# Matmul with batch norm on one core: the shift column, the fifth tile's first blocks and the last tile's first chunk

## The chip, the cores and the metric

The kernel runs on one core of a Trainium2 chip. A core has a matrix engine (TensorE, PE in the profile), three engines for elementwise work (VectorE or DVE, ScalarE or ACT, GpSimd or POOL), a queue engine that issues transfers (SyncE, SP) and 16 DMA engines that move data between memory and the core. SBUF is the core's working memory, and PSUM the memory of eight banks into which TensorE writes. The metric is the device time of one execution in microseconds (us); lower is better.

## The reference

```python
y = np.matmul(x, weight)                       # x: 16 x 512 x 1024, weight: 1024 x 768
mean = np.mean(y, axis=(0, 1), keepdims=True)  # over all 8192 rows, one value per column
var = np.var(y, axis=(0, 1), keepdims=True)
y_norm = (y - mean) / np.sqrt(var + eps)
return (gamma * y_norm + beta).astype(np.float32)
```

No output can be written before the mean and the variance of its column are known, that is, before all 8192 rows of that column are multiplied. The output is 8192 x 768 floats, 25.17 MB.

## The kernel before, in words

The 768 columns are six tiles of 128, counted `nt` = 0 to 5 (`NT` = 6), and the 8192 rows are 16 chunks of 512, counted `c` (`C` = 16). While x is loaded, the first three tiles (`GA` = 3) are computed for all chunks, and tiles 3, 4 and 5 for the first five chunks (`EARLY` = 5). Once x is in, tiles 3, 4 and 5 follow one after the other for chunks 5 to 15 (line 579 on): eight matmuls of 128 x 512 for each chunk (`mm`, line 196). This is the part that the change touches.

In tiles 3 to 5 a product lies with the columns of y on the partitions. For each chunk VectorE takes the statistics from PSUM (`bn`, line 318) and ScalarE copies the product to SBUF as bf16 (`keep`, line 345). Both read the same bank, and ScalarE's copy waits for VectorE's statistics. When a tile's last chunk is through, `finish_var` (lines 352 to 354) and `finish_affine` (lines 358 to 363) make the tile's scale and shift: VectorE aggregates, ScalarE takes the root, VectorE the reciprocal, ScalarE makes scale and shift by three operations of one element per partition, and, in line 363, copies the shift to a spare column of a PSUM bank. That bank (`a_ps`, line 270) also holds the scale row that VectorE multiplies the first three tiles with (`norm_rows`, line 285). Tile 3 has column 384 of the bank and tile 4 column 385.

Then the outputs of the tile (`outputs`, line 547) go through in blocks of two chunks (b = 0 to 7):

- `norm` multiplies by scale and adds shift in place. It has three forms. "act" is one ScalarE activation (line 381). "dve" is a VectorE `tensor_scalar` (line 392). "dve1" is a VectorE `scalar_tensor_tensor` that reads the shift from the PSUM column (line 387). While GpSimd still works on the first three tiles' rows (`shift_rows`, line 291), the even chunk of a block goes to ScalarE and the odd one to VectorE as "dve1"; later blocks are all "dve".
- `turn_y` queues eight 128 x 128 transposes on TensorE (line 408). Inside the matmul loop one waiting transpose is issued after each matmul (`turn_one`), and whatever is left when the block is copied out is issued in one burst (`out_copy`).
- `out_copy` has ScalarE copy the transposed block from PSUM to SBUF as float (line 421), and `store` issues a 512 KB store on SyncE's queue (line 426).

Tile 4's last block is held back (`HELD` = 1) until tile 5's matmuls are issued. Tile 5, the last, is finished by `finish` (line 366). Its chunks then go out one by one (`last_outputs`, line 568): normalise on VectorE, four transposes, one ScalarE copy of 128 x 512, one store of 256 KB.

The order of the work on each engine is fixed when the program is built. `at(t, fn, ...)` notes a step with a planned time, the list is sorted by these times, and `seq` chains the instructions of each engine in that order. An instruction that waits therefore holds everything that stands behind it on its engine. The planned times are no measurement; they only set the order. The framework adds the waits between engines from what each instruction reads and writes.

Of the kernel before, what the change touches and what calls it, by code (L numbers as in the profile page):

```python
# [10 lines left out]
def kernel(  # L11
# [23 lines left out]
    nc = tc.nc  # L35
# [3 lines left out]
    ALU = mybir.AluOpType  # L39
# [5 lines left out]
    P = 128  # L45
    NT = N // P
    KQ = K // 4
    CH = 512
    RT = CH // P
    C = M // CH  # L50
    QR = 256
    QPC = CH // QR
# [5 lines left out]
    GA = 3  # L58
    COLS = (0, 5, 10, 15)
    NA = GA * P  # L60
# [16 lines left out]
    def seq(bi):  # L77

        ins = bi.ins
        prev = last.get(ins.engine)  # L80
        if prev is not None:
            tc.add_manual_dep(
                ins, prev,
                mybir.DependencyInfo(mybir.DependencyClass.NoSync, mybir.DependencyReason.DATA),
                reason="order",
            )
        last[ins.engine] = ins.name
        return bi
# [6 lines left out]
    scale = singles.tile([P, NT], f32)  # L95
    shift = singles.tile([P, NT], f32)
# [30 lines left out]
    xs, xT, py, ygrp, yrow, ops, ost, aff = {}, {}, {}, {}, {}, {}, {}, {}  # L127
# [140 lines left out]
    def spread_rows(i):  # L268

        a_ps = psum.tile([P, CH], f32, tag="b")  # L270
        aff[i] = a_ps[:, 0:NA]
        if i == 0:
            aff["shift"] = a_ps[:, NA:NA + NT - GA]
        seq(nc.tensor.matmul(aff[i], full, aff["diag"][:, i], start=True, stop=True))  # L274
        if i == 1:
            seq(nc.scalar.copy(sum1, aff[i]))  # L276
# [24 lines left out]
    def y(nt, c):  # L301
        key, i = ((nt, c // GY), c % GY) if nt >= GA else ((0, c), nt)
        if key not in ygrp:
            y_sb = ypool.tile([P, GY, CH], bf16, tag="y")
            ygrp[key] = y_sb
        return ygrp[key][:, i]
# [49 lines left out]
    def finish_affine(nt):  # L356
        one = slice(nt, nt + 1)
        seq(nc.scalar.activation(nscale, rstd, AF.Identity, scale=ngamma[:, one]))
        seq(nc.scalar.activation(scale[:, one], rstd, AF.Identity, scale=gamma_sb[:, one]))
        seq(nc.scalar.activation(  # L360
            shift[:, one], mv[:, nt, 0:1], AF.Identity, bias=beta_sb[:, one], scale=nscale))
        if nt < NT - 1:
            seq(nc.scalar.copy(aff["shift"][:, nt - GA:nt - GA + 1], shift[:, one]))

    def finish(nt):
        one = slice(nt, nt + 1)
# [12 lines left out]
    def norm(nt, c, eng):  # L379
        if eng == "act":  # L380
            seq(nc.scalar.activation(  # L381
                y(nt, c), y(nt, c), AF.Identity,
                bias=shift[:, nt:nt + 1], scale=scale[:, nt:nt + 1],
            ))
        elif eng == "dve1":

            seq(nc.vector.scalar_tensor_tensor(  # L387
                y(nt, c), y(nt, c), scale[:, nt:nt + 1],
                aff["shift"][:, nt - GA:nt - GA + 1].to_broadcast([P, CH]), op0=ALU.mult, op1=ALU.add,
            ))  # L390
        else:
            seq((nc.vector if eng == "dve" else nc.gpsimd).tensor_scalar(  # L392
                y(nt, c), y(nt, c), scale[:, nt:nt + 1], shift[:, nt:nt + 1],
                op0=ALU.mult, op1=ALU.add,
            ))

    def turn_y(nts, m0, tiles):

        o_ps = psum.tile([P, tiles, len(nts), P], bf16, tag="b")
        ops[nts, m0] = o_ps  # L400
        for s in range(tiles):
            c, i = divmod(m0 // P + s, RT)
            for a, nt in enumerate(nts):
                turns.append(((nts, m0), o_ps[:, s, a], y(nt, c)[:, i * P:(i + 1) * P]))
# [30 lines left out]
    def at(t, fn, *args):  # L435
        events.append((t, len(events), fn, args))
# [85 lines left out]
    at(S + 0.9, affine_rows)  # L522
    at(S + 2.4, shift_diag)
    at(S + 4.4, spread_rows, 0)
    at(S + 5.6, spread_rows, 1)
    for nt in range(GA):
        at(S + 5.0, norm, nt, 0, "dve")
    ga = tuple(range(GA))
    tr, tk = S + 4.7, S + 6.3
    for c in range(C):  # L530
        if c in COLS:
            for nt in range(GA):
                if c:
                    at(tk - 3.4 + 0.8 * nt, norm, nt, c, "act")
            for s in range(0, RT, 2):
                at(tk + 0.7 * s, turn_y, ga, c * CH + s * P, 2)
                at(tk + 0.7 * s + 1.9, out_copy, ga, c * CH + s * P, "act")
                at(tk + 0.7 * s + 2.7, store, ga, c * CH + s * P, 2)
            tk += 9.6 if c else 7.2
        else:  # L540
            for s in range(0, RT, 2):
                at(tr, norm_rows, c, s)
                at(tr + 1.1, shift_rows, c, s)
                at(tr + 3.0, store_rows, c, s)
                tr += 1.85

    def outputs(nt, t0, step):
        for b in range(C // 2):
            tb = t0 + step * b
            if nt == NT - 2 and b >= C // 2 - HELD:  # L550
                held.append(b)
                continue
            for i in range(2):
                at(tb - 2.2 + 0.5 * i, norm, nt, 2 * b + i, "dve" if tb > tr + 2.0 else "dve1" if i else "act")
            at(tb, turn_y, (nt,), 2 * b * CH, 2 * RT)
            at(tb + 2.2, out_copy, (nt,), 2 * b * CH, "act")
            at(tb + 2.3, store, (nt,), 2 * b * CH, 2 * RT)
# [10 lines left out]
    def last_outputs(nt, t0):  # L568

        for c in range(C):  # L570
            tb = t0 + 0.6 * c
            at(tb - 1.2, norm, nt, c, "dve")
            at(tb, turn_y, (nt,), c * CH, RT)
            at(tb + 0.5, out_copy, (nt,), c * CH, "act", True)
            at(tb + 0.6, store, (nt,), c * CH, RT)
# [3 lines left out]
    for nt in range(GA, NT):  # L579
        for c in range(EARLY, C):  # L580
            if (nt, c) == (NT - 1, C - 1):
                for q in range(QPC):
                    at(pe, mm_half, q)
                    pe += 0.9
                    at(pe + 0.2, bn_half, q)
                    at(pe + (0.4 if q == 0 else 1.0), keep_half, q)
                at(pe - 2.4, sum_up)
                continue
            for jws in halves:
                unit(nt, c, MM_US / 2 + (0.12 if nt == GA else 0.17), jws)  # L590
        if nt < NT - 1:
            at(pe + 0.55, finish_var, nt)
            at(pe + 1.6, finish_affine, nt)
        else:
            at(pe + 0.55, finish, nt)
        if nt == GA:
            outputs(nt, S + 37.0, 2.3)
        elif nt < NT - 1:
            outputs(nt, pe + 4.6, 1.85)
        else:  # L600
            held_outputs(nt - 1, pe)
            last_outputs(nt, pe + 3.0)
# [39 lines left out]
```

## Time and profile before

| | us |
|---|---|
| four runs | 217.39, 217.95, 218.10, 218.62; median 218.03 |
| the profiled execution | 217.39, its span 215.6 |
| PE busy in the span | 200.8 (93%) |
| DVE busy | 152.2 (71%) |
| POOL busy | 133.8 (62%) |
| ACT busy | 120.6 (56%) |
| loading and the first three tiles' matmuls | to about 124 |
| tiles 3 to 5, the rest of their matmuls | to about 197 |
| after the last matmul to the end of the span | about 18 |

The span is from the first to the last instruction; 1.79 us of the profiled execution lie around it. A busy PE is not a PE at its peak, since matmuls overlap. What counts in the stretch from 124 to 197 us is the distance between the starts of the PE's instructions: 0.28 us for a matmul of 128 x 512 with a transpose behind it. In the last 18 us the DMA engines write the last tile. The profile gives starts, durations and, in brackets, how long an engine sat idle ahead of an instruction and which instruction released it.

### The profile page before, as it was taken

How to read it: one execution, taken by the hardware profiler on the slowest of the kernel's cores; microseconds unless marked ns; L12 is line 12 of the kernel's file. 1: busy time of each engine (PE TensorE's matmuls, PEld its weight loads, DVE VectorE, ACT ScalarE, POOL GpSimd, SP SyncE). 2: the span in 40 equal slices, each digit the busy share in tenths (PEclk: the TensorE clock that was granted, in tenths of full speed). 3: DMA queues.
4: the chain of work that ended last, by engine and by line, in shares of the span. 5: the costliest groups of instructions: out<-in, count | busy, mean ns of one | idle time of the engine just before them, and what ended most of it. 6: DMA issues, size and time to landing. Idle time of an engine off the chain costs nothing.

```text
span 215.6 us, 3455 instructions
## 1 busy us (share of the span) xinstructions
PE 200.8 (93%) x1178; PEld 106.4 (49%) x1178; DVE 152.2 (71%) x263; ACT 120.6 (56%) x229; POOL 133.8 (62%) x153
## 2 busy tenths in 40 slices
PE   7998999999999999999999999999999999996900
PEld 2453555554544566645656544444445545554900
DVE  3222868897988789998754449988999949838800
ACT  2001463654553466645666423867768977996950
POOL 7788677779684699962558402999999943000000
PEclk9999999999999999999999999999999999999675
DMA  4999999999999999996000000598789998999997
GB/s 55 170 200 182 196 196 192 197 194 195 196 190 194 197 196 196 196 197 83 0 5 0 0 0 0 204 383 310 287 297 367 362 338 283 303 347 325 303 345 233
DMA packets 70161, 43.75 MB, mean 203 GB/s; under 512 B 4096, under 2 KB 69632, under 8 KB 70144
## 3 DMA queue, kind: packets, MB, share of 16 engines
q0 software_dynamic: 34624, 18.36, 62.1%
q1 hardware_dynamic: 35520, 25.18, 36.1%
q8 instruction: 9, 0.15, 0.3%
q14 instruction: 8, 0.07, 0.1%
HBM read 36.71 MB, written 25.17 MB: 287 GB/s over the span
## 4 chain that ended last, share of the span: by engine, by line
PE 78%; ACT 5%; DMA 5%; DVE 3%; POOL 3%; issue 1%; ACTq 0%; POOLq 0%
PE y_ps L196 43%; PE y_ps L186 29%; PE o_ps L408 4%; ACT o_sb L421 3%; DMA w_sb<-in_weight_dram 3%; DMA ring<-in_x_dram 2%; POOL w_sb L149 2%; POOL ring L162 1%; ACT ring L421 1%; PE y_ps L332 1%; ACT y_sb L381 1%; DVE stats L318 1%; DVE y_sb L387 1%; PE a_ps L274 1%; PE tot_ps L232 1%
## 5 line engine op out<-in xcount | busy, mean ns | idle before, releaser
L196 PE MATMUL y_ps<-xT_sb,w_sb 128*128 128x512 bf16 (+1 forms) x484 | 117.5, 382 | 1.1 <-DMA w_sb<-in_weight_dram 0.8
L196 PEld LDWEIGHTS <-w_sb 128*128 128x128 bf16 x484 | 46.0, 96 | 59.2 <-issue 2.7
L345 ACT CAST y_sb<-y_ps 128x512 bf16<-128x512 f32 x59 | 35.1, 595 | 51.3 <-DVE stats L318 48.4
L186 PE MATMUL y_ps<-w_sb,xT_sb 128*128 128x384 bf16 x384 | 63.4, 326 | 0.0
L162 POOL DMA_DIRECT2D ring<-in_x_dram x72 | 45.2, 634 | 12.5 <-DVE xT_sb L174 6.5
L318 DVE BATCH_NORM_STATS2 stats<-y_ps 128x6 f32<-128x512 f32 x58 | 39.1, 685 | 17.6 <-PE y_ps L196 17.6
L186 PEld LDWEIGHTS <-xT_sb 128*128 128x128 bf16 x384 | 37.6, 98 | 25.6
L174 DVE STREAM_TRANSPOSE xT_sb<-ring 128x1024 f32<-128x1024 f32 (+1 forms) x34 | 39.5, 1170 | 14.3 <-DMA ring<-in_x_dram 14.2
L212 POOL TENSOR_TENSOR sum<-sum,sq_sb 128x384 f32<-128x384 f32 x38 | 38.1, 1002 | 17.4 <-ACT sq_sb L208 15.9
L408 PE MATMUL o_ps<-ident,y_sb 128*128 128x128 bf16 x240 | 38.8, 230 | 2.1 <-DVE y_sb L392 1.7
L291 POOL TENSOR_TENSOR ring<-ring,sum 128x768 f32<-128x768 f32 x17 | 31.0, 1847 | 12.1 <-ACT sum L276 12.1
L215 DVE TENSOR_TENSOR sum<-y_ps,sum 128x384 f32<-128x384 f32 x48 | 26.1, 545 | 13.9 <-ACT sq_sb L208 12.9
L208 ACT ACTIVATE sq_sb<-y_ps 128x384 f32<-128x384 f32 x48 | 23.5, 494 | 13.8 <-PE y_ps L186 10.5
L221 ACT CAST y_sb<-y_ps 128x384 bf16<-128x384 f32 x48 | 22.9, 478 | 9.4 <-DVE sum L215 9.2
L421 ACT CAST ring<-o_ps 128x1024 f32<-128x1024 bf16 (+1 forms) x24 | 22.9, 972 | 4.4 <-PE o_ps L408 2.3
L408 PEld LDWEIGHTS <-y_sb 128*128 128x128 bf16 x240 | 21.0, 103 | 5.5 <-DVE y_sb L392 1.8
L285 DVE TENSOR_TENSOR ring<-y_sb,a_ps 128x768 f32<-128x768 bf16 x17 | 15.9, 939 | 0.0
L291 POOL TENSOR_TENSOR o_sb<-o_sb,sum 128x768 f32<-128x768 f32 x7 | 12.8, 1833 | 4.0 <-DVE o_sb L285 4.0
L381 ACT ACTIVATE y_sb<-y_sb,shift,scale 128x512 bf16<-128x512 bf16 x17 | 13.5, 816 | 0.0
L392 DVE TENSOR_SCALAR y_sb<-y_sb,scale,shift 128x512 bf16<-128x512 bf16 x35 | 12.5, 421 | 0.0
L155 PE MATMUL idle_ps<-idle_sb 128*128 128x512 bf16 x38 | 11.0, 458 | 1.2 <-DVE idle_sb L103 1.2
L421 ACT CAST o_sb<-o_ps 128x512 f32<-128x512 bf16 x16 | 7.9, 673 | 0.3 <-PE o_ps L408 0.3
(64 smaller groups left out, 56.2 us busy)
## 6 DMA issues: line engine op xcount, KB each, us to landing
ring<-in_x_dram POOLq DMA_DIRECT2D x56, 256.0 KB, 8.6
out_dram<-ring SPq DMA_DIRECT2D x25, 384.0 KB, 3.4
out_dram<-ring SPq DMA_DIRECT2D x16, 512.0 KB, 4.2
out_dram<-o_sb SPq DMA_DIRECT2D x16, 256.0 KB, 3.9
out_dram<-o_sb SPq DMA_DIRECT2D x7, 384.0 KB, 3.7
ring<-in_x_dram POOLq DMA_DIRECT2D x16, 128.0 KB, 5.3
w_sb<-in_weight_dram POOLq DMA_DIRECT2D x8, 96.0 KB, 4.6
w_sb<-in_weight_dram POOLq DMA_DIRECT2D x4, 192.0 KB, 5.1
```

Of the source, the lines that this page charges most:

```text
L162: seq(nc.gpsimd.dma_start(x_bf[32 * i:32 * i + 32], src[:, :, KQ * i:KQ * (i + 1)]))
L174: seq(nc.vector.transpose(dst[:, half, :, jw0:jw1], src[:, :, jw0:jw1]))
L186: seq(nc.tensor.matmul(y_ps, xT[c][:, jw, s * P:(s + 1) * P, e], w_sb[:, jw, e, 0:NA], start=(jw == 0 and e == 0), stop=(jw == JW - 1 and ...
L196: seq(nc.tensor.matmul(y_ps, w_sb[:, jw, e, nt * P:(nt + 1) * P], xT[c][:, jw, q0 * QR:q1 * QR, e], start=(jw == 0 and e == 0 and q0 == 0) ...
L208: seq(nc.scalar.activation(sq_sb, py["row", c, s][:, 0:NA], AF.Square))
L212: seq(eng.tensor_add(acc, acc, py.pop(("sq", c, s))))
L215: seq(nc.vector.tensor_add(sum1, py["row", c, s][:, 0:NA], sum1))
L291: seq(nc.gpsimd.tensor_add(o_sb, o_sb, sum1[:, None, :].to_broadcast([P, 2, NA])))
L318: seq(nc.vector.bn_stats(stats_of(nt)[:, i, :], py[nt, c]))
L345: seq(nc.scalar.copy(y(nt, c), py.pop((nt, c))))
L408: seq(nc.tensor.transpose(dst, src, ident))
L421: seq(nc.scalar.copy(o_sb, src))
```

## The change

It has three parts.

1. The shift in PSUM. ScalarE's copy of the shift (line 363), made for tiles 3 and 4, goes away. For tile 3 alone VectorE copies its shift to the one PSUM column that is left (`shift_to_psum`); the step is planned just ahead of the tile's first norms.
2. Tile 4's first blocks. The odd chunk of an early block is "dve1" only for tile 3. For tile 4 it becomes "act". Only block 0 is early enough for this, so one chunk, c = 1, moves from VectorE to ScalarE.
3. The last tile's first chunk. Instead of one norm of 512, four transposes, one copy of 512 and one store of 256 KB there are two halves, each with a norm of 256, two transposes, a copy of 256 and a store of 128 KB.

```diff
@@ spread_rows
-            aff["shift"] = a_ps[:, NA:NA + NT - GA]
+            aff["shift"] = a_ps[:, NA:NA + 1]
@@ finish_affine
-        if nt < NT - 1:
-            seq(nc.scalar.copy(aff["shift"][:, nt - GA:nt - GA + 1], shift[:, one]))
@@ norm, "dve1"
-                aff["shift"][:, nt - GA:nt - GA + 1].to_broadcast([P, CH]), op0=ALU.mult, op1=ALU.add,
+                aff["shift"].to_broadcast([P, CH]), op0=ALU.mult, op1=ALU.add,
+
+    def shift_to_psum(nt):
+        seq(nc.vector.tensor_copy(aff["shift"], shift[:, nt:nt + 1]))
+
+    def norm_half(nt, c, q):
+        part = y(nt, c)[:, q * QR:(q + 1) * QR]
+        seq(nc.vector.tensor_scalar(
+            part, part, scale[:, nt:nt + 1], shift[:, nt:nt + 1], op0=ALU.mult, op1=ALU.add))
@@ outputs
+        if nt == GA:
+            at(t0 - 2.3, shift_to_psum, nt)
-                at(tb - 2.2 + 0.5 * i, norm, nt, 2 * b + i, "dve" if tb > tr + 2.0 else "dve1" if i else "act")
+                at(tb - 2.2 + 0.5 * i, norm, nt, 2 * b + i, "dve" if tb > tr + 2.0 else "dve1" if i and nt == GA else "act")
@@ last_outputs
+            if c == 0:
+
+                for q in range(QPC):
+                    at(tb - 1.2, norm_half, nt, c, q)
+                    at(tb, turn_y, (nt,), q * QR, RT // QPC)
+                    at(tb + 0.4 + 0.1 * q, out_copy, (nt,), q * QR, "act", True)
+                    at(tb + 0.4 + 0.1 * q, store, (nt,), q * QR, RT // QPC)
+                continue
```

## The prediction

> **What bounds the kernel now.** I first read the busy slices of the page. PE is full from the start of the matmuls to about 197 us, and the DMA engines are full from 184 us to the end. So two stretches matter: where PE stalls before 197 us, and what starts the last run of the DMA. For the first I read the chain that ended last (start, duration, what):
>
> ```profile
> 173.24 0.13 ACT std L353
> ...
> 176.31 0.17 ACT a_ps L363
> 176.51 0.76 DVE y_sb L387
> 177.31 0.23 PE o_ps L408
> ...
> 179.40 0.72 ACT y_sb L381
> 180.16 0.23 PE o_ps L408
> ```
>
> Twice in the turn from tile 4's statistics to its outputs the chain leaves PE: at 177.31 a transpose waits for a VectorE norm that waits for ScalarE's shift copy, and at 180.16 one waits for a ScalarE norm. Elsewhere between 133 and 195 us it goes matmul after matmul. The two engines' timelines show why. VectorE:
>
> ```profile
> 173.57 0.16 DVE L354 RECIPROCAL rstd<-std 128x1 f32<-128x1 f32 x1 [0.36 <-ACT std L353]
> 176.51 0.75 DVE L387 SCALAR_TENSOR_TENSOR y_sb<-y_sb,scale,a_ps 128x512 bf16<-128x512 bf16 x1 [2.77 <-ACT a_ps L363]
> 177.17 0.69 DVE L318 BATCH_NORM_STATS2 stats<-y_ps 128x6 f32<-128x512 f32 x1
> ```
>
> By the order of instructions the norm at 176.51 is tile 3's chunk 11. It needs tile 3's shift, ready since 151 us. It sits 2.77 us because tile 4's shift goes to the next column of the same PSUM tile ahead of it: a wait for the tile, not for the data. The statistics behind it (tile 5's chunk 5, whose matmuls ended near 173.3) come at 177.17, so late that ScalarE waits for them in turn:
>
> ```profile
> 175.90 0.38 ACT L360 ACTIVATE shift<-mv,beta_sb,nscale 128x1 f32<-128x1 f32 x1
> 176.31 0.16 ACT L363 COPY a_ps<-shift 128x1 f32<-128x1 f32 x1
> 176.41 0.81 ACT L381 ACTIVATE y_sb<-y_sb,shift,scale 128x512 bf16<-128x512 bf16 x1
> 177.90 0.59 ACT L345 CAST y_sb<-y_ps 128x512 bf16<-128x512 f32 x1 [0.68 <-DVE stats L318]
> 178.38 1.02 ACT L421 CAST ring<-o_ps 128x1024 f32<-128x1024 bf16 x1
> 179.28 0.83 ACT L381 ACTIVATE y_sb<-y_sb,shift,scale 128x512 bf16<-128x512 bf16 x1
> 181.50 0.59 ACT L345 CAST y_sb<-y_ps 128x512 bf16<-128x512 f32 x1 [1.39 <-DVE stats L318]
> ```
>
> The norm at 176.41 is tile 4's chunk 0, that at 179.28 is tile 3's chunk 12; it stands behind the copy at 177.90. For the end I read windows of a quarter microsecond (PE, PEld, DVE, ACT, POOL busy with counts, PE clock, DMA share, GB/s):
>
> ```profile
> 198.75:199.00 0.25, 0.00 (x0) 0.00 (x0) 0.21 (x2) 0.25 (x1) 0.00 (x0) 1.00 1.18 344
> ...
> 199.75:200.00 0.25, 0.25 (x5) 0.15 (x5) 0.25 (x2) 0.23 (x1) 0.00 (x0) 1.00 0.08 25
> ...
> 200.25:200.50 0.25, 0.25 (x7) 0.20 (x4) 0.25 (x3) 0.25 (x2) 0.00 (x0) 1.00 1.14 346
> ```
>
> The DMA is dry from about 199.1 to 200.2, then runs at some 346 GB/s to about 213.85 without a hole. That run carries 4.5 MB (2^20 bytes each): tile 4's held block of 512 KB, then tile 5's sixteen stores. 4.72e6 bytes / 346 GB/s = 13.64 us, and 200.2 + 13.64 = 213.84. So its start alone sets the end. The timeline gives what starts it:
>
> ```profile
> 198.22 0.99 ACT L421 CAST ring<-o_ps 128x1024 f32<-128x1024 bf16 x1
> ...
> 199.23 0.37 SPq L426 DMA_DIRECT2D out_dram<-ring  x1
> ...
> 200.38 0.37 SPq L426 DMA_DIRECT2D out_dram<-o_sb  x1
> ```
>
> The held block's store is issued at 199.23 and its data flow at 200.2, 0.97 us later. Its 524288 bytes last 1.51 us, to 201.7. Tile 5's first store, issued at 200.38, can flow from 201.35 and waits behind it.
>
> **What the skill says.** The Trainium skill, "ScalarE: Activation LUTs", section "Rules for kernel authors", budgets about 0.3 us for an ACTIVATE plus 0.83 ns an element, an estimate of 0.72 us for 512. The trace agrees: norms start 0.70 to 0.72 us apart. "GPSIMD Engine Reference", "Specifications", says that GpSimd shares its SBUF interfaces with VectorE's two-port modes. The trace agrees: the VectorE norm of line 392 that met a GpSimd add at 179.95 took 0.91 us against a mean of 0.42. "DMA: Bandwidth & Descriptors", "Latency and other measured facts", gives about 0.6 us to the first byte; with the 0.37 us of issue that makes 0.97, as above.
>
> **Part 1, the shift column.** Removed are two ScalarE copies of 0.16 us. The one at 151.40 lies in front of a wait of 0.38 us and is worth nothing. The one at 176.31 holds the next norm by 0.10 us (176.31 to 176.41). With it goes VectorE's wait: the changed order of instructions has no ScalarE wait left on chunk 11's norm. VectorE then runs, by start distances in this timeline (norm 0.65, statistics 0.61, row product 0.86): chunk 11 from about 173.66, statistics 174.31, row product 174.92, chunk 13 at 175.78, tile 4's chunk 2 at 176.43, when the shift (176.28) is there. PE's stalls against its own rhythm are 177.31 - 176.83 = 0.48, 0.09 in the burst at 179.30 (0.37 instead of 0.28 to the next matmul; it waited for chunk 1 on VectorE), and 180.16 - 179.90 = 0.26. Together 0.83 us is the most that this place can give.
>
> Added is VectorE's copy of 128 x 1 near 160.9 us, with a wait of the norm behind it. No such copy is in the trace. Its neighbours of one element take 0.15 to 0.16 us; with the wait I take 0.2, bounds 0.08 and 0.4. Queued behind it are norms, row products and the statistics that ScalarE waits for. Those statistics wait for PE at 162.51, 166.79 and 169.04 with gaps of 0.12, 0.05 and 0.13 us, together 0.30, which hide it. Without that cover ScalarE's later turn starts up to 0.2 us later, and what is gained at 180 us is lost.
>
> **Part 2, chunk 1 on ScalarE.** VectorE loses 0.65 us, which nobody waits for any more. ScalarE gains 0.71 us ahead of everything that follows. Its work from 173.24 to 176.28 is unchanged and back to back, so: chunk 0 at 176.31, chunk 1 at 177.02, copy of tile 5's chunk 5 at 177.73 (statistics ready near 175, no wait now), the 128 x 1024 copy at 178.21, tile 3's chunk 12 at 179.11, done 0.83 later at 179.94; PE can transpose it at 179.99. PE itself would be there at 180.16 - 0.83 = 179.33. So ScalarE sets it, and PE gains 180.16 - 179.99 = 0.17 us of the 0.83. Behind this point PE ran without a stall to 195.25 although ScalarE was back to back from 181.50 to 192.98. ScalarE now comes 1.67 us earlier (its copy at 181.50 moves to 179.83), so it cannot be the next limit. The statistics it needs then are late next: tile 4's chunk 2 meets GpSimd's add, moved up to about 176.0 to 177.9, and those statistics end near 178.6, 1.2 us early. Stores of tiles 3 and 4 are issued up to 1.7 us earlier on SP; their DMA work ends earlier and the dry spell before 200 us grows. It costs nothing.
>
> **Part 3, the halves.** Seen alone they bring the first store forward: a VectorE norm of 256 saves some 0.06 us, two transposes fewer 0.11, and the ScalarE copy of 256 takes 0.37 (line 342's row of that size) instead of 0.59, so 0.4 in all: issue at 199.98. But tile 5's first data wait behind the held block until 201.7, 0.35 us after they could flow. Worth nothing; 0.4 if that cover were gone. Added are one SP issue (0.37 to 0.83 us, median 0.54), one ScalarE copy and one PSUM bank, while ScalarE ends at 207.7 and the DMA at 213.85. The total of bytes and the 512-byte rows stay.
>
> **Sum.** -0.17 from PE, shifting all that follows, 0 from the halves: 217.39 - 0.17 = 217.22 for the profiled execution, the lowest of the four. On their median, 0.64 above it, 217.86.
>
> **Rivals.** (a) ScalarE is not the limit: chunk 12 is ready early, as if its queue ran half a microsecond faster. PE gains up to 0.83 us: 217.2. For it: the chain names the shift copy first. Against: each start distance on ScalarE is measured and repeats. (b) The first store counts after all, because the held block leaves a hole. 0.17 + 0.4: 217.45. Against: no window after 200.25 shows one. (c) Slower: half stores starve the DMA. 128 KB flow in 0.38 us, an issue can take 0.83, so two can leave 2 x 0.83 - 0.76 = 0.9 us dry: 217.86 + 0.9 = 218.76. It decides when the held block's 1.51 us no longer cover it, that is if the third store is issued after 201.35 (flow of the halves ends near 202.3, less 0.97). I expect about 201.0. (d) The wait at 173.7 stays in another form. Then ScalarE's extra 0.71, less the copy's 0.10, fills its idle 0.68 at 177.90 and nothing moves: 218.03.
>
> **How the numbers follow.** My case 0.55, (a) 0.13, (b) 0.12, (c) 0.08, (d) 0.12. About 0.5% (1.09 us) is what a measurement can tell from no change. No case alone reaches it. The four runs spread by 1.2 us, and (a) with (b) would reach 1.2, so I give 0.09 to faster and 0.06 to slower, most of that from (c) and from stalls I do not see. The range reaches from (a) less some scatter, 216.9, to just below (c), 218.6.
>
> **What would show it.** Right: VectorE's wait of 2.77 us is gone, tile 5's chunk 5 statistics come near 174.3, PE flows through 177, and one stall of about 0.6 us remains at the first transpose of chunk 12, released by ScalarE. The last matmul comes some 0.2 us earlier, tile 5's first store some 0.6 us earlier, and the DMA still starts with the held block near 200.0. Wrong: no stall left at chunk 12 (a), a dry window after 201 us (c), or the end moving by more than the last matmul (b).

## The result and the profile after

The changed kernel takes 217.64 us (median of 43 runs) against 218.10 us (64 runs) before. The ratio is 0.998, with a 95% interval of 0.9969 to 0.9991, that is -0.44 us (-0.68 to -0.20). The profiled execution took 217.07 us with a span of 215.3 us.

Absolute times in two profiles don't compare well, because what lies ahead of the stretch takes longer in one execution than in another. So I count from one event: the start of the root of tile 4's variance (line 353), at 173.24 us before and 173.33 us after (172.67 to 174.55 us over all thirteen profiles). Times after the change carry this offset of 0.09 us.

The chain that ended last, after the change (start, duration, what):

```profile
179.04 0.29 PE o_ps L414 x5
179.36 0.66 ACT y_sb L379
180.06 0.23 PE o_ps L414
```

Before, the chain left PE twice in this turn, at 177.31 and 180.16. Now it leaves it once, for the ScalarE norm of tile 3's chunk 12. VectorE's timeline after the change:

```profile
173.65 0.16 DVE L354 RECIPROCAL rstd<-std 128x1 f32<-128x1 f32 x1 [0.36 <-ACT std L353]
173.73 0.73 DVE L385 SCALAR_TENSOR_TENSOR y_sb<-y_sb,scale,a_ps 128x512 bf16<-128x512 bf16 x1
174.38 0.69 DVE L318 BATCH_NORM_STATS2 stats<-y_ps 128x6 f32<-128x512 f32 x1
176.50 1.59 DVE L390 TENSOR_SCALAR y_sb<-y_sb,scale,shift 128x512 bf16<-128x512 bf16 x1
```

The norm of tile 3's chunk 11 no longer sits behind tile 4's shift: counted from the root it starts 2.87 us earlier (176.51 - 173.73, and 0.09), and the statistics that ScalarE needs start 2.88 us earlier. The last line is tile 4's chunk 2, which meets GpSimd's add and takes 1.59 us. ScalarE after the change:

```profile
175.98 0.38 ACT L360 ACTIVATE shift<-mv,beta_sb,nscale 128x1 f32<-128x1 f32 x1
176.40 1.52 ACT L379 ACTIVATE y_sb<-y_sb,shift,scale 128x512 bf16<-128x512 bf16 x2
177.82 0.56 ACT L345 CAST y_sb<-y_ps 128x512 bf16<-128x512 f32 x1
178.29 1.01 ACT L427 CAST ring<-o_ps 128x1024 f32<-128x1024 bf16 x1
179.19 0.82 ACT L379 ACTIVATE y_sb<-y_sb,shift,scale 128x512 bf16<-128x512 bf16 x1
179.91 0.57 ACT L345 CAST y_sb<-y_ps 128x512 bf16<-128x512 f32 x1
```

Both idle times of before (0.68 and 1.39 us) are gone. The line at 176.40 now holds two norms, chunks 0 and 1 of tile 4, and chunk 12 at 179.19 stands behind them. PE waits for it:

```profile
180.06 0.23 PE L414 MATMUL o_ps<-ident,y_sb 128*128 128x128 bf16 x1 [0.52 <-ACT y_sb L379]
```

The matmul ahead of this transpose started at 179.16. By PE's rhythm before the change, 0.23 us from a matmul to the transpose behind it, it was due at 179.39, so PE loses 0.67 us.

The end, in quarter microseconds after the change (busy time and count of PE, PEld, DVE, ACT, POOL; PE clock; DMA share; GB/s):

```profile
198.75:199.00 0.25, 0.00 (x0) 0.00 (x0) 0.23 (x1) 0.25 (x1) 0.00 (x0) 1.00 0.14 43
...
199.50:199.75 0.25, 0.21 (x2) 0.04 (x3) 0.25 (x2) 0.25 (x1) 0.00 (x0) 1.00 0.01 2
199.75:200.00 0.25, 0.25 (x4) 0.22 (x4) 0.25 (x2) 0.25 (x2) 0.00 (x0) 1.00 0.00 0
...
200.25:200.50 0.25, 0.25 (x6) 0.15 (x4) 0.25 (x2) 0.25 (x1) 0.00 (x0) 0.91 1.14 346
```

The DMA's last run starts near 200.05 us. Just ahead of it the rate is really zero. Before the change 45 and then 25 GB/s still trickled in the half microsecond to 200.00 us.

### The profile page after: what moved, and what is told of

Read it like the earlier page. It is cut to its first block, busy times and chain, and to the rows that moved or that the text cites. A ratio compares the mean times of both kernels' runs of the same rounds, so it can differ in the third digit from the quotient of the medians.

```text
span 215.3 us, 3459 instructions
## 1 busy us (share of the span) xinstructions
PE 200.4 (93%) x1178; PEld 106.5 (49%) x1178; DVE 152.4 (71%) x264; ACT 121.2 (56%) x229; POOL 133.9 (62%) x153
## 4 chain that ended last, share of the span: by engine, by line
PE 85%; DMA 5%; POOL 3%; ACT 1%; issue 1%; DVE 1%; ACTq 0%; POOLq 0%
PE y_ps L196 47%; PE y_ps L186 29%; PE o_ps L414 7%; DMA w_sb<-in_weight_dram 2%; DMA ring<-in_x_dram 2%; POOL w_sb L149 2%; POOL ring L162 1%; ACT o_sb L427 1%; PE y_ps L332 1%; PE a_ps L274 1%; PE tot_ps L232 1%; ACT y_sb L379 0%; ACTq L653 0%; DVE fin L339 0%; DVE y_sb L400 0%
## 5 line engine op out<-in xcount | busy, mean ns | idle before, releaser
L345 ACT CAST y_sb<-y_ps 128x512 bf16<-128x512 f32 x59 | 34.5, 585 | 49.7 <-DVE stats L318 46.8
L208 ACT ACTIVATE sq_sb<-y_ps 128x384 f32<-128x384 f32 x48 | 23.5, 495 | 11.2 <-PE y_ps L186 8.4
L379 ACT ACTIVATE y_sb<-y_sb,shift,scale 128x512 bf16<-128x512 bf16 x18 | 14.2, 815 | 0.0
L427 ACT CAST o_sb<-o_ps 128x512 f32<-128x512 bf16 (+1 forms) x17 | 8.1, 632 | 0.2
```

The costliest lines, as they stand in the source:

```text
L208: seq(nc.scalar.activation(sq_sb, py["row", c, s][:, 0:NA], AF.Square))
L345: seq(nc.scalar.copy(y(nt, c), py.pop((nt, c))))
L427: seq(nc.scalar.copy(o_sb, src))
```

## The experiments

Three theories are tested. A and B compete; C came later, for what A leaves open.

**A**: ScalarE's added norm holds PE at chunk 12, so only 0.17 to 0.19 us of the 0.83 that the shift column sets free come through; the halves are hidden behind the held block's store.

**B**: the halves carry what the matmuls don't explain of the 0.44 us.

**C** (formed later): the earlier stores of tiles 3 and 4 are worth something of their own.

The table has one profile each, as distances: from tile 4's root to the start of tile 5's last matmuls (line 332 of the kernel before), from there to the end of the last output packet in the trace, and their sum, in us. They are read from times of two decimals, so the last digit can be off by one. The last column is the timed ratio to the kernel before.

| kernel | root to last matmuls | to last packet | sum | ratio (95%) |
|---|---|---|---|---|
| before | 22.01 | 18.86 | 40.87 | |
| the change | 21.82 | 18.70 | 40.52 | 0.998 (0.9969 to 0.9991) |
| e1 no halves | 21.83 | 18.69 | 40.52 | 0.9989 (0.9968 to 1.001) |
| e2 halves alone | 22.01 | 18.82 | 40.83 | 0.9999 (0.9978 to 1.002) |
| e3 chunk 12 on VectorE | 21.14 | 18.69 | 39.83 | 0.9962 (0.9944 to 0.9979) |
| e4 chunk 1 on VectorE | 21.13 | 18.69 | 39.82 | 0.9959 (0.994 to 0.9979) |
| e5 none held | 21.58 | 18.32 | 39.90 | 0.9963 (0.9946 to 0.9979) |
| e6 none held, halves | 21.58 | 18.25 | 39.83 | 0.9939 (0.9918 to 0.9961) |
| e7 more ScalarE work | 22.42 | 18.69 | 41.11 | 1.001 (0.9996 to 1.0024) |
| e8 chunk 1 on VectorE, halves | 21.14 | 18.70 | 39.84 | 0.9946 (0.9925 to 0.9966) |
| e9 late copies | 21.92 | 19.06 | 40.98 | 0.9994 (0.9975 to 1.0014) |
| e10 as e5 | 21.58 | 18.32 | 39.90 | 0.9944 (0.9923 to 0.9964) |
| e11 as e6 | 21.57 | 18.25 | 39.82 | 0.9937 (0.9912 to 0.9963) |

### e1 and e2: the halves left out, and the halves alone

e1, against the changed kernel:

```diff
@@ last_outputs
-            if c == 0:
-
-                for q in range(QPC):
-                    ...
-                continue
```

> The change without its third part (the last tile's first chunk stays whole). Theory A (ScalarE limits at chunk 12 of tile 3; the halves are hidden behind the held block's store): the same as the full change, -0.2 us against before; the DMA's last run still starts with the held block, about 1.0 us after its issue, without a hole behind it. Theory B (the halves carry the part of the measured -0.4 us that the matmuls do not explain): about 0.2 to 0.3 us slower than the full change, so -0.1 to -0.2 against before, with a hole in the DMA behind the held block.

e2, against the kernel before:

```diff
+    def norm_half(nt, c, q):
+        ...
@@ last_outputs
+            if c == 0:
+                for q in range(QPC):
+                    at(tb - 1.2, norm_half, nt, c, q)
+                    ...
+                continue
```

> Only the third part on the kernel before. Theory A: 0.0 us against before; the first store of the last tile is issued 0.4 to 0.5 us earlier (near 199.9 instead of 200.4) and the end does not move. Theory B: -0.2 to -0.4 us.

Without the halves the distances are those of the full change to 0.01 us, 0.9989 timed. The halves alone leave the first distance where it was, and the second within 0.04 us of it, 0.9999 timed. In e2 the first store is issued 4.74 us after the last matmuls begin (201.30 - 196.56) against 5.13 before (200.38 - 195.25), so it does come 0.39 us earlier and is hidden. This is what theory A says, and it speaks against B. The timed intervals alone, some 0.9 us wide, would not have settled it.

### e3 and e4: who does the norm

e3, against the changed kernel, gives chunk 12 of tile 3 to VectorE:

```diff
-... "dve1" if i and nt == GA else "act")
+... "dve1" if nt == GA and (i or b == 6) else "act")
```

> The full change, and tile 3's chunk 12 is normalised by VectorE (the form that reads the shift from PSUM) instead of ScalarE. Theory A: the stall of 0.62 us at 180.06 is gone, the last matmul comes 0.6 us earlier than in the full change, the DMA's last run starts 0.6 us earlier too, so about -0.6 us against the full change and -0.8 to -1.0 against before. Theory B, or one in which the DMA sets the end on its own: the matmuls move, the end does not, -0.2 to -0.4 against before.

e4, against e1, gives tile 4's chunk 1 back to VectorE, reading the shift from SBUF:

```diff
-... "dve1" if i and nt == GA else "act")
+... ("dve1" if nt == GA else "dve") if i else "act")
```

> Part one alone: VectorE copies tile 3's shift, ScalarE's two copies are gone, tile 4's chunk 1 stays on VectorE but reads the shift from SBUF, and the first chunk of the last tile is whole. Theory A: without the added ScalarE norm chunk 12 is ready at about 179.3 and PE does not stall at all: 0.83 us of the turn come free and the end moves by -0.8 us against before. Chunk 1 meets GpSimd's add and takes some 1.6 us on VectorE, which nobody waits for. Rival: that collision delays chunk 1, chunk 13 and the statistics behind them, PE stalls at chunk 1's or chunk 13's transposes, and no more than 0.2 us is gained.

Both take the stall away. The last matmuls come 0.68 and 0.69 us earlier than in the full change, and the end follows by 0.69 and 0.70. This is what shows the cause: two different edits that each relieve ScalarE's queue by one norm give the same 0.7 us. VectorE in e3 takes chunks 13 and 12 in one go (first line below), and in e4 the moved norm waits for the shift and then for GpSimd's add, which ran from 176.39 to 178.23:

```profile
176.14 1.40 DVE L385 SCALAR_TENSOR_TENSOR y_sb<-y_sb,scale,a_ps 128x512 bf16<-128x512 bf16 x2
```

```profile
176.69 1.69 DVE L390 TENSOR_SCALAR y_sb<-y_sb,scale,shift 128x512 bf16<-128x512 bf16 x1 [0.47 <-ACT shift L360]
178.30 0.73 DVE L385 SCALAR_TENSOR_TENSOR y_sb<-y_sb,scale,a_ps 128x512 bf16<-128x512 bf16 x1
```

The norm's 1.69 us cost nothing: among the waits of e4 between 173 and 182 us there is none of PE. Against before e4 gains 0.88 us in matmul distance and 1.05 in all, more than the 0.83 that I had as the most. The timed -0.89 us (-1.31 to -0.46) covers both.

### e7: more work for ScalarE

Against the changed kernel, extra work behind chunk 1; the result goes to a tile that nobody reads any more:

```diff
@@ norm, "act"
+            if (nt, c) == (NT - 2, 1):
+                seq(nc.scalar.activation(
+                    sum3, sum3, AF.Identity,
+                    bias=shift[:, nt:nt + 1], scale=scale[:, nt:nt + 1],
+                ))
```

> The full change, and behind tile 4's chunk 1 ScalarE does one more activation, of 128 x 384 floats into a tile that nobody reads any more (extra work; about 0.6 us from one start to the next). Theory A (ScalarE's queue sets the stall at chunk 12): the stall grows from 0.62 to about 1.2 us, the last matmul comes 0.6 us later than in the full change and the end too, so +0.3 to +0.4 us against before. Rival (the stall is there for another reason and ScalarE has room): no change against the full change, -0.2 to -0.4 against before.

ScalarE in e7, and PE at chunk 12:

```profile
177.25 0.69 ACT L384 ACTIVATE sum<-sum,shift,scale 128x384 f32<-128x384 f32 x1
177.85 0.56 ACT L345 CAST y_sb<-y_ps 128x512 bf16<-128x512 f32 x1
```

```profile
180.09 0.23 PE L419 MATMUL o_ps<-ident,y_sb 128*128 128x128 bf16 x1 [1.11 <-ACT y_sb L379]
```

The extra activation takes 0.60 us of the queue, the matmul distance grows by 0.60 as well, from 21.82 to 22.42, and the second distance stays. PE's idle time there goes from 0.52 to 1.11. The timed +0.22 us (-0.09 to +0.52) has the interval around zero, so here the profile decides.

### e5, e6, e8, e10, e11: the held block as cover

e5 and e6 are built on e4, e6 with the halves:

```diff
-    HELD = 1
+    HELD = 0
```

> Part one with chunk 1 on VectorE (as in the run that kept chunk 1 there), and no block of tile 4 is held back; the last tile's first chunk is whole. Now its store starts the DMA's last run. Theory A (the start of that run alone sets the end): PE gets eight transposes more before its last matmul, +0.45 us; the run starts with the first store, issued some 1.15 us after the last matmul than the held store was, +1.15; it carries 512 KB less, -1.51. Together +0.1 us against the kernel with the held block, -0.7 to -0.8 against before. Rival (the tail is bound by something behind the start, such as ScalarE's copies or SP's issues): +0.5 or more against the kernel with the held block.

> The same without a held block, and with the first chunk in two halves. Theory A: with the cover gone the halves are worth what they bring the first store forward, 0.4 us: -0.4 against the same kernel with a whole first chunk, -1.1 to -1.2 against before, the fastest of all. Rival (two stores of 128 KB leave the DMA dry between them): a window below 300 GB/s within the first 1.5 us of the run, and no gain.

e8 is e4 with the halves and with the held block:

> Part one with chunk 1 on VectorE, a block held back, and the first chunk in two halves. Theory A: as without the halves, -0.8 us against before, since the held block still covers them. Theory B (the halves carry something of their own): -1.0 to -1.2 against before.

e10 and e11 are e5 and e6 once more:

> The kernel with chunk 1 on VectorE, no held block and a whole first chunk, once more beside its sibling with halves. By its first profile the end comes 39.90 us after tile 4's root, 0.97 us before that of the kernel before; -0.8 to -1.0 us.

> The same with the first chunk in halves. If the profile is right (the run starts 0.41 us earlier, but the DMA runs thin for 0.34 us between the halves): 0.1 us faster than the sibling, -0.9 to -1.1 against before. If the first timing is right: 0.4 to 0.5 us faster than the sibling, -1.2 to -1.4.

With the held block the halves move nothing: e8 and e4 agree to 0.02 us in the profile. By the timing e8 lies 0.0013 below e4, inside both intervals.

In e5 PE pays 0.45 us for the eight transposes (21.13 to 21.58), as expected. The last run then starts 6.04 us after the last matmuls begin, with the first store, instead of 4.90, and has 512 KB less to carry; the second distance falls from 18.69 to 18.32. Together +0.08 against e4.

In e6 the halves do bring the run forward, to 5.63 us, by 0.41. But the end gains only 0.07. Windows of e6 (columns as above):

```profile
200.00:200.25 0.25, 0.25 (x5) 0.25 (x4) 0.25 (x2) 0.25 (x2) 0.00 (x0) 0.50 1.15 350
200.25:200.50 0.25, 0.25 (x5) 0.25 (x4) 0.25 (x2) 0.25 (x2) 0.00 (x0) 0.50 0.48 135
200.50:200.75 0.25, 0.25 (x5) 0.25 (x3) 0.25 (x2) 0.25 (x2) 0.00 (x0) 0.50 1.12 340
200.75:201.00 0.25, 0.25 (x5) 0.25 (x4) 0.25 (x2) 0.25 (x2) 0.00 (x0) 0.50 0.45 127
```

After each half the DMA runs thin, because the stores are issued half a microsecond apart (198.99, 199.45, 199.97) and a half lasts 0.38 us. The second issue waits for SyncE, which is busy with the first to 199.36; for the third SyncE (to 199.88) and ScalarE's copy (to 199.87) come free together. Against 346 GB/s the windows to 201.25 lack 0.33 us, which is the 0.41 less what came through. So the hole of the prediction's rival (c) exists, but only once the cover is gone. The expectation for e6, -0.4 us from the halves, is wrong by the profile. The timing says -0.5 us in the first pair and -0.15 us in the second, with wide intervals. The profile's 0.07 to 0.08 us repeats in both pairs, the timed difference does not, so what the halves are worth on the timed median is not settled.

e3, e4, e5, e6 and e8 are all faster than the kernel before. Against the change their profiles gain 0.62 to 0.70 us; by the timing only e6 and e8, and the repeats e10 and e11, have intervals clear of its own. e6 and e11 have the lowest ratios, 0.9939 and 0.9937, but their intervals overlap those of e4 and e8.

### e9: the stores late again

The matmuls explain 0.19 us of the change, but the profile's sum fell by 0.35. The second distance is 18.82 to 18.86 in the two kernels with the old shift copy, and 18.69 to 18.70 in six others that hold a block, with halves or without. What these six share is that ScalarE copies tile 4's blocks earlier. e9 undoes this alone, on the full change:

```diff
@@ norm, "act"
+            for n in (NA, NA, P) if (nt, c) == (GA, 12) else ():
+                seq(nc.scalar.activation(
+                    sum3[:, 0:n], sum3[:, 0:n], AF.Identity,
+                    bias=shift[:, nt:nt + 1], scale=scale[:, nt:nt + 1],
+                ))
```

> The full change, with three ScalarE activations into a tile that nobody reads any more (384, 384 and 128 floats wide, extra work, about 1.8 us together) right behind the norm of chunk 12, so that ScalarE's copies of tile 4's blocks and their stores come as late as before the change. Nothing that PE waits for at chunk 12 is later. Theory C (earlier stores are worth something of their own: two of the 16 DMA engines finish their share some 1.5 us after the others, before the change only just as the last run starts): the matmuls end as in the full change, 21.8 us after tile 4's root, but the last bytes land 18.8 to 18.9 us after the last tile's last matmuls begin instead of 18.7; against before -0.2 us, against the full change +0.15. Rival (the drain is without effect): 18.7, as in the full change, -0.35 against before.

ScalarE's copy behind chunk 12 moves to 8.45 us after the root (181.47 - 173.02), where it was at 8.26 before the change and at 6.58 after it. PE's first distance rises only by 0.10, to 21.92, which I have not followed further. The second rises to 19.06. Ahead of the last run and at the end of the DMA work in e9:

```profile
199.25:199.50 0.25, 0.25 (x2) 0.07 (x2) 0.25 (x2) 0.22 (x1) 0.00 (x0) 1.00 0.07 23
199.50:199.75 0.25, 0.21 (x4) 0.22 (x4) 0.25 (x2) 0.25 (x2) 0.00 (x0) 1.00 0.07 20
...
213.50:213.75 0.25, 0.00 (x0) 0.00 (x0) 0.00 (x0) 0.00 (x0) 0.00 (x0) 0.50 0.25 70
213.75:214.00 0.25, 0.00 (x0) 0.00 (x0) 0.00 (x0) 0.00 (x0) 0.00 (x0) 0.50 0.07 20
```

and at the end of the full change:

```profile
213.50:213.75 0.25, 0.00 (x0) 0.00 (x0) 0.00 (x0) 0.00 (x0) 0.00 (x0) 0.50 1.06 316
213.75:214.00 0.25, 0.00 (x0) 0.00 (x0) 0.00 (x0) 0.00 (x0) 0.00 (x0) 0.50 0.09 21
```

A sixteenth of 346 GB/s is 21.6. In e9 about that much still runs right up to the last run, and again after it, alone, for some 0.4 us. In the full change everything is quiet ahead of the run, and the main flow itself is the last thing to end.

The packets of the stores, counted one by one in the traces, give the size. The last run begins 4.90 us after the last matmuls begin. From then on, 13 packets of 512 bytes more than the run's own 9216 are written in the kernel before, 11 in e2 and 21 in e9, and not one in the six kernels at 18.69 to 18.70. Ahead of the run the late ones come 23.5 ns apart, one behind the other, as from a single engine, and so do the last packets of all three kernels. At that pace 13, 11 and 21 packets take 0.31, 0.26 and 0.49 us; the last packet lands 0.16, 0.13 and 0.36 us later than in the six. The difference is 0.13 to 0.15 us each time.

This is theory C: late stores push a part of one DMA engine's work into the last run, and the end waits for that engine. It also gives the reason why e9 lost 0.36 us where I expected 0.15: its copies are 0.19 us later than before the change, and eight packets more are left. e3 is the test from the other side: about 20 GB/s run there until 0.2 us before the last run, and cost nothing. Which engine it is the trace does not name. The timed -0.13 us of e9 (-0.55 to +0.31) fits, but does not decide.

## Why the prediction was right, and where its size was off

The forecast was no measurable change with -0.17 us as its likeliest value. Measured was -0.44 us (-0.68 to -0.20), inside the range and inside the 0.5%, but with the -0.17 just outside the interval. What happens at PE was forecast step by step. But nearly half of what the profile gained came from a term that I had put at nothing, and that this term was small enough to leave the forecast standing is luck.

**Part 1.** Right. The wait was one for the PSUM tile: it is gone with the write to the neighbouring column. VectorE takes chunk 11 0.08 us after the reciprocal starts, and the statistics start at 174.38, expected at 174.31 plus the offset of 0.09. The VectorE copy took 0.15 us and moved the norm behind it by 0.19, for which I had 0.2. The gaps hid it: the statistics at 169.12 have the same offset of 0.08 as those at 160.36, ahead of the copy.

**Part 2.** Right, step by step. Chunk 12 was to be ready at 179.94 and ended at 180.01, that is 179.92 without the offset. PE stood 0.67 us (expected 0.66), and the last matmuls came 0.19 us earlier (expected 0.17). The 0.83 us that I called the most this place can give was a little low: e4 got 0.88. e3, e4 and e7 show the cause from both sides. The collision of tile 4's chunk 2 with GpSimd came as stated, and its statistics ended at 178.70.

**Part 3.** Right for the kernel as it is: 0.39 us earlier, hidden. The price I gave should the cover be gone, 0.4 us, was wrong: e6 and e11 give 0.07 to 0.08, since two short stores don't keep the DMA full.

**The step that failed** is the sentence on the stores of tiles 3 and 4: "their DMA work ends earlier and the dry spell before 200 us grows. It costs nothing." I had called the DMA dry from 199.1 us although the windows that I quoted showed 25 GB/s. That remainder reached into the last run, so the start of that run alone did not set the end: the last packet before the change landed at 214.11 us (195.25 + 18.86), not near 213.85. Ending the remainder earlier was worth 0.16 us (18.86 to 18.70). With it the sum is 0.19 + 0.16 = 0.35, inside the measured interval.

**The rivals.** (a) is what e3 and e4 made of the kernel, not what the change did. (b) and (c) did not occur behind the held block. The sign that I had named for (b), the end moving by more than the last matmuls, did appear (0.35 against 0.19 us), but e1 and e2 show that the halves are not its cause and e9 shows what is: the sign was too wide. (The sum under (b) should read 217.46.) (d) fell with VectorE's wait.

## What to carry to other kernels

Work that is moved off an engine which waits lands on the queue of another, and there it can count in full for everything behind it: the added norm, 0.71 us of ScalarE's queue, ate 0.69 of the 0.88 us that the same change set free. So before moving an instruction, look at what the receiving engine does next and who waits for it; here VectorE had the room, as e3 and e4 show.

A low transfer rate is not an empty queue: read what is left over in front of a run that sets the end.

Two half stores bring the end forward only if each flows long enough to cover the issue of the next; here 0.38 us of flow stood against half a microsecond.

## What the runs showed that I had not expected

The stores do not drain evenly. After the main flow of tile 4's stores ends, 43 to 45 GB/s, about two sixteenths of 346, go on for a microsecond (198.00 to 199.00 us in the full change), then about one sixteenth. The DMA share in these windows, 0.14 and 0.07 against 1.15 at full flow, says the same. The last run itself, nearly 14 us long, ends evenly (316, 21 and 0 GB/s in the three quarter microseconds from 213.50 us), so it is not that some engines write more slowly all the time.

The traces hold a reason for one of the late engines. Besides the stores there are packets of 16 KB on a DMA queue that the profile calls "instruction" (q8). One of them falls into tile 4's last stores in all thirteen profiles and takes 0.93 to 0.96 us, in the full change from 196.39 to 197.33 us. Windows ahead of it and within it (columns as above):

```profile
196.00:196.25 0.25, 0.25 (x4) 0.21 (x3) 0.07 (x1) 0.14 (x1) 0.00 (x0) 1.00 1.16 352
...
196.50:196.75 0.25, 0.25 (x5) 0.20 (x3) 0.19 (x1) 0.22 (x2) 0.00 (x0) 1.00 1.09 330
```

While it lasts, the stores flow at 324 to 328 GB/s in every profile, about one sixteenth below the full rate, as if one engine fetched instructions instead of storing. Each store closes with sixteen packets of 4 bytes. In the kernel before, one of the sixteen comes 0.6 us behind the others in nine stores in a row up to this fetch. In the store that is under way during the fetch a second one is late, by 1.25 us, and that one reaches into the last run. This is read from the traces alone: no run moved or removed the fetch, and why the other engine is late stays open.

The Trainium skill, "DMA: Bandwidth & Descriptors", section "Latency and other measured facts", says that DMA engines 7 and 15 are usually slower than the others and ties this, as a best guess, to transfers issued by GpSimd. Here the lag is on SyncE's stores, and which engines it is no run here shows.
